# Attention on one Trainium2 core: transposed weights and value products on two shared PSUM buffers, two tiles of queries at a time

## The chip, the cores and the metric

The kernel runs on one core of a Trainium2 chip. The metric is device time in microseconds (us) of that core for one execution of the whole two-layer network; the profile is one further execution, recorded by the hardware profiler. Engines: PE multiplies matrices (PEld is its weight load), DVE is the vector engine, ACT the scalar engine, POOL the general engine, SP issues most DMAs. Each engine runs its instructions in the order of its own queue.

## The reference

Layer 0 is a gated DeltaNet and an S5 scan, layer 1 is attention; a mixture of experts follows each. The change is in the attention of layer 1, which the reference computes so, for three pairs of window and dilation that are merged by their softmax denominators:

```python
scores = einsum('bdnqhe,bdnkhe->bdhnqk', qb, kk) * (e ** -0.5)     # 16 heads of 64, 1024 tokens
scores = where(valid, scores, -1e30)
m = max(scores, -1);  p = exp(scores - m);  ssum = sum(p, -1)
out = einsum('bdhnqk,bdnkhe->bdnqhe', p / ssum, vv);  lse = m + log(ssum)
...
o = einsum('cbsh,cbshe->bshe', softmax(stack(lses)), stack(outs))
y = o @ w_out                                                      # then residual, LayerNorm, experts
```

The kernel merges the three branches into one causal softmax by adding to each score the logarithm of the number of branches that hold the pair (the table `amask`).

## The kernel before

`attention` works on 8 pairs of heads, 8 tiles of 128 queries each, and the two heads of a pair: 128 steps `u`, with a pair's tiles in the order `IORD` = 0, 7, 1, 6, 2, 5, 3, 4. A step with tile `i` has `n = 128 * (i + 1)` keys. The work on PE is written out by hand (`manual_schedule` for PE); the order on the other engines comes from a scheduler that follows a model of the program. Each pass of the loop at L1044 emits:

- `transposed(u)`: the softmax weights `sm` of step `u` (128 queries by `n` keys) are transposed 128 columns at a time (L988) into a PSUM bank `pp`, up to four to a bank. A tile `i > 3` needs two banks full. ACT copies the first to SBUF (`pt`, L992), DVE the second (L994). After each bank come *fillers*: 3 matmuls where `i > 3`, 6 otherwise.
- `out(u - 2)`, at even `u`: the product of values and transposed weights for both heads of a tile (L1007), 2(i + 1) matmuls of 64 columns of weights (the profile has two records for each), into a PSUM bank `po` of its own. ACT copies it to `yt` (L1013); for the last pair ACT and DVE split it into two parts (`olast`, L449 and L450).
- `weights(u + 4)`: scores of step `u + 4` (L965, L967) into a PSUM tile `s`; DVE adds the mask and takes the maximum (L971, L974), ACT exponentiates (L975), DVE divides by the sum (L976, L977).

The fillers are a generator: first the projections of queries and keys of the next pairs (`qk`, L1088, into banks `pj`, with their weight DMAs and copies on ACT, DVE and POOL). They run out in step 108, pair 6. When pair 6 is through (`done`, step 112), the output weights `wo1` are split on ACT and POOL (L1030) with no PE work, and from step 124 on the product with them (L1038) fills again. PSUM has 8 banks, all in use: `s` 2 x 2, `pj` 2, `pp` 1, `po` 1. SBUF tiles `pt` have 3 buffers.

Behind attention, `out_stage` multiplies by `wo1`, normalises and routes; its tables `og`, `ob`, `owr`, `ogb`, `orb` (L191, L233, L236) are loaded by SP. Then 32 experts stream 192 MB of weights (`wraw`, L458), and `combine` ends the program.

Of the kernel before, what the change touches and what calls it, by code (L numbers as in the profile page):

```python
# [10 lines left out]
F32 = mybir.dt.float32  # L11
# [10 lines left out]
NT = 8  # L22
# [29 lines left out]
AH = 4  # L52
# [101 lines left out]
class Trunk:  # L154
# [788 lines left out]
    def attention(self, xTh, xTl, xp, V, ytd, ps, wp):  # L943

        nc = self.nc
        self.banks = {"pj": 2}
        ps.tile([128, D], F32, name="s", tag="s")
        am = wp.tile([128, 1024], F32, name="amask", bufs=1)  # L950
        nc.sync.dma_start(am, self.I["amask"])
        lo_half, hi_half = slice(0, 64), slice(64, 128)
        steps = [(pr, i, a) for pr in range(8) for i in IORD for a in range(2)]
        pairs, P, yts = {}, {}, {}
        with self.pool("at", 2) as ap, self.tc.manual_schedule(engines={mybir.EngineType.PE}):

            def weights(u):
                pr, i, a = steps[u]
                n = 128 * (i + 1)
                QS, KH, KL = pairs[pr]  # L960
                s = ps.tile([128, D], F32, name="s", tag="s")
                w = 256 if n < 256 else 768 if n == 640 else n
                cuts = [0, w] if w <= 512 else [0, 512, w]
                for c0, c1 in zip(cuts[:-1], cuts[1:]):
                    nc.tensor.matmul(s[:, c0:c1], QS[a][:, i * 128:(i + 1) * 128], KH[a][:, c0:c1],  # L965
                                     start=True, stop=False)
                    nc.tensor.matmul(s[:, c0:c1], QS[a][:, i * 128:(i + 1) * 128], KL[a][:, c0:c1],  # L967
                                     start=False, stop=True)
                sm = ap.tile([128, D], F32, name="sm", tag="sm", bufs=AH)
                st = ap.tile([128, 4], F32, name="st", tag="st", bufs=AH + 1)  # L970
                nc.vector.tensor_tensor_reduce(  # L971
                    out=sm[:, :n], in0=s[:, :n], in1=am[:, 1024 - n:1024], scale=1.0, scalar=-3e38,
                    op0=OP.add, op1=OP.max, accum_out=st[:, 0:1])
                nc.vector.tensor_scalar(st[:, 1:2], st[:, 0:1], -1.0, None, op0=OP.mult)  # L974
                nc.scalar.activation(sm[:, :n], sm[:, :n], AF.Exp, bias=st[:, 1:2], accum_out=st[:, 2:3])  # L975
                nc.vector.reciprocal(st[:, 3:4], st[:, 2:3])  # L976
                nc.vector.tensor_scalar(sm[:, :n], sm[:, :n], st[:, 3:4], None, op0=OP.mult)  # L977
                P[u] = sm

            def transposed(u):  # L980
                _, i, a = steps[u]
                sm = P[u]
                pt = ap.tile([128, NT, 128], F32, name="pt", tag="pt", bufs=3)
                for j0 in range(0, i + 1, 4):
                    j1 = min(j0 + 4, i + 1)
                    pp = ps.tile([128, 512], F32, name="pp", tag="pp", bufs=1)
                    for j in range(j0, j1):
                        nc.tensor.transpose(pp[:, (j - j0) * 128:(j - j0 + 1) * 128],  # L988
                                            sm[:, j * 128:(j + 1) * 128], self.ident)
                    v = pp[:, :(j1 - j0) * 128].rearrange("p (j q) -> p j q", q=128)  # L990
                    if j0 == 0:
                        nc.scalar.activation(pt[:, j0:j1], v, AF.Copy)  # L992
                    else:
                        nc.vector.tensor_copy(pt[:, j0:j1], v)  # L994
                    for _ in zip(range(3 if i > 3 else 6), fill):
                        pass
                P[u] = pt

            def out(u):

                pr, i, _ = steps[u]
                if i == IORD[0] and pr < 7:
                    yts[pr] = ap.tile([128, D], F32, name="yt", tag="yt")
                po = ps.tile([128, 512], F32, name="po", tag="o", bufs=1)
                for j in range(i + 1):
                    for a, h in enumerate((lo_half, hi_half)):
                        nc.tensor.matmul(po[h, :128], V[:, j, (2 * pr + a) * 64:(2 * pr + a + 1) * 64],  # L1007
                                         P[u + a][:, j], start=(j == 0), stop=(j == i))
                ts = slice(i * 128, (i + 1) * 128)
                if pr == 7:  # L1010
                    self.split(po[:, :128], O["last"][0][:, ts], O["last"][1][:, ts])
                    return
                nc.scalar.activation(yts[pr][:, ts], po[:, :128], AF.Copy)  # L1013
                if i == IORD[-1]:
                    nc.sync.dma_start(ytd[pr], yts[pr])
                    done.add(pr)

            def fillers():
                yield from self.qk(pairs, xTh, xTl, ap, wp)
                xp.release()  # L1020
                op = O["pool"] = self.tc.alloc_tile_pool(name="ow1", bufs=1, side="right", reuse_waits="tile")
                O["last"] = [op.tile([128, D], F32R, name=f"olast{i}") for i in range(2)]
                while 6 not in done:
                    yield
                raws = [ap.tile([128, D], F32, name="oraw", tag=t) for t in ("QS0", "QS1", "KL1")]
                raw = [raws[k % 3] for k in range(KT)]
                W = O["W"] = []
                for k in range(KT):
                    nc.sync.dma_start(raw[k], self.I["wo1"][k])
                    W.append(self.out_weights(k, raw[k], op, nc.gpsimd))  # L1030
                    yield from [None] * WPACE
                y, yh, yl = (ap.tile([128, KT - 1, 128], F32 if t == "KH0" else F32R, name="y0", tag=t)
                             for t in ("KH0", "KH1", "KL0"))
                nc.sync.dma_start(y, ytd[:, :, 0:128].rearrange("k p t -> p k t"))
                self.split(y, yh, yl)
                O["y"] = [(yh[:, k], yl[:, k]) for k in range(KT - 1)]
                O["po"] = [self.bank("po0", "pj") for _ in range(2)]
                yield from self.out_products(O["po"], O["y"], W, range(KT - 1))  # L1038

            O, done = {}, set()  # L1040
            fill = fillers()
            for _ in zip(range(96), fill):
                pass
            for u in range(-AH, len(steps) + 2):  # L1044
                if 0 <= u < len(steps):
                    transposed(u)
                elif u < 0:
                    for _ in zip(range(6), fill):
                        pass
                if u >= 2 and u % 2 == 0:  # L1050
                    out(u - 2)
                if u + AH < len(steps):
                    weights(u + AH)
            for _ in fill:
                pass
            for _ in self.out_products(O["po"], O["y"] + [[t[:, 0:128] for t in O["last"]]], O["W"], [KT - 1]):
                pass
        return O["W"], O["last"], O["po"], ps, O["pool"]
# [1035 lines left out]
```

## Time and profile before

| | |
|---|---|
| median of 3 runs | 2521.05 us (2517.41 to 2521.86) |
| profiled execution | 2522.76 us, its span 2520.9 us |
| granted TensorE clock, mean | 0.957 of 2.4 GHz |
| PE, DVE, ACT busy over the span | 2276.8, 1466.6, 1146.6 us |
| stretch of the 128 steps | 1364 us to 1781 us |

Times in the rows count from the span's start. A PE row's length holds the pipeline's depth, so that matmuls overlap in the rows: what a matmul costs is the distance from its start to the next one's start.

### The profile page before, as it was taken

How to read it: one execution, taken by the hardware profiler on the slowest of the kernel's cores; microseconds unless marked ns; L12 is line 12 of the kernel's file. 1: busy time of each engine (PE TensorE's matmuls, PEld its weight loads, DVE VectorE, ACT ScalarE, POOL GpSimd, SP SyncE). 2: the span in 40 equal slices, each digit the busy share in tenths (PEclk: the TensorE clock that was granted, in tenths of full speed). 3: DMA queues.
4: the chain of work that ended last, by engine and by line, in shares of the span. 5: the costliest groups of instructions: out<-in, count | busy, mean ns of one | idle time of the engine just before them, and what ended most of it. 6: DMA issues, size and time to landing. Idle time of an engine off the chain costs nothing. (4 is left out here: it accounts for less than half of the span.)

```text
span 2520.9 us, 33905 instructions
## 1 busy us (share of the span) xinstructions
PE 2276.8 (90%) x11950; PEld 1629.8 (65%) x11950; DVE 1466.6 (58%) x2901; ACT 1146.6 (45%) x1871; POOL 485.0 (19%) x566
## 2 busy tenths in 40 slices
PE   7999999899697999998599999997996979999986
PEld 5888888678454555555477777775784545555552
DVE  7655656556853555554554766766468535555545
ACT  5436353442453444443324666666325534444432
POOL 1445433102231111110001111103113311111100
PEclk9999999899798999999799999998997989999997
DMA  4222222272599999999531000102725999999986
GB/s 162 61 64 50 57 79 68 102 272 86 220 365 401 411 404 402 400 399 390 178 124 34 30 31 26 41 24 83 270 74 206 375 398 410 405 405 407 401 334 252
DMA packets 179198, 560.82 MB, mean 222 GB/s; under 512 B 59200, under 2 KB 96448, under 8 KB 129360
## 3 DMA queue, kind: packets, MB, share of 16 engines
q1 hardware_dynamic: 163920, 525.01, 55.1%
q0 software_dynamic: 15104, 33.60, 3.6%
q8 instruction: 96, 1.57, 0.2%
q14 instruction: 78, 0.64, 0.1%
HBM read 518.76 MB, written 55.36 MB: 228 GB/s over the span
## 5 line engine op out<-in xcount | busy, mean ns | idle before, releaser
L489 DVE TENSOR_TENSOR wlo<-wraw,whi 128x1024 fp32r<-128x1024 f32 x380 | 447.8, 1220 | 139.9 <-ACT whi L486 136.9
L486 ACT ACTIVATE whi<-wraw 128x1024 fp32r<-128x1024 f32 x384 | 384.4, 1053 | 76.2 <-PE pu L529 36.2
L583 PE MATMUL pgs<-wraw,xs 128*64 128x512 f32 x1024 | 241.3, 603 | 0.0
L583 PEld LDWEIGHTS pgs<-wraw,xs 128*64 128x64 f32 x1024 | 70.1, 138 | 133.4 <-issue 129.9
L172 PE MATMUL pj<-xTh,phi 128*128 128x512 f32 x320 | 131.9, 417 | 13.6 <-ACT xTh L449 13.6
L1072 POOL TENSOR_TENSOR plo<-praw,phi 128x256 fp32r<-128x256 f32 x64 | 50.2, 786 | 437.6 <-ACT phi L1071 291.4
L172 PE MATMUL pj<-xTh,plo 128*128 128x512 f32 x320 | 132.5, 415 | 0.0
L172 PE MATMUL pj<-xTl,phi 128*128 128x512 f32 x320 | 131.1, 410 | 0.0
L971 DVE CUSTOM_DVE_ANT_0 sm<-s,amask 128x1024 f32<-128x1024 f32 (+7 forms) x128 | 96.6, 756 | 51.5 <-PE s L967 49.6
L528 PE MATMUL pg<-whi,xh 128*128 128x512 f32 x256 | 107.0, 418 | 18.9 <-ACT whi L486 13.8
L599 PE MATMUL pos<-wraw,hs 128*64 128x512 f32 x512 | 118.6, 598 | 5.7 <-ACT xh L449 3.3
L988 PE MATMUL pp<-cf,sm 128*128 128x128 f32 x576 | 100.8, 285 | 22.8 <-ACT pt L992 18.0
L172 PE MATMUL opo<-ohi,oyp 128*128 128x512 f32 x392 | 115.7, 403 | 2.4 <-DVE oyp L450 2.4
L1088 PE MATMUL pj<-xTh,phi 128*128 128x512 f32 x256 | 114.6, 448 | 2.9 <-ACT phi L1071 1.0
L528 PE MATMUL pg<-wlo,xh 128*128 128x512 f32 x256 | 108.2, 423 | 8.1 <-DVE wlo L489 7.8
L551 POOL DMA_INDIRECT yd<-ot,first x32 | 38.0, 1188 | 369.2 <-issue 178.8
L975 ACT ACTIVATE sm<-sm,st 128x1024 f32<-128x1024 f32 (+7 forms) x128 | 99.1, 775 | 18.7 <-DVE st L974 16.4
L988 PEld LDWEIGHTS pp<-cf,sm 128*128 128x128 f32 x576 | 68.4, 143 | 57.8 <-ACT pt L992 50.0
L528 PE MATMUL pg<-whi,xl 128*128 128x512 f32 x256 | 103.4, 404 | 0.0
L529 PE MATMUL pu<-wlo,xh 128*128 128x512 f32 x256 | 102.4, 400 | 0.0
L529 PE MATMUL pu<-whi,xl 128*128 128x512 f32 x256 | 102.3, 400 | 0.0
L529 PE MATMUL pu<-whi,xh 128*128 128x512 f32 x256 | 102.2, 399 | 0.0
(543 smaller groups left out, 5195.7 us busy)
## 6 DMA issues: line engine op xcount, KB each, us to landing
wraw<-in_wm SPq DMA_DIRECT2D x384, 1024.0 KB, 8.3
cy<-yd SPq DMA_DIRECT2D x32, 512.0 KB, 7.3
praw<-in_win SPq DMA_DIRECT2D x40, 256.0 KB, 2.7
oraw<-in_wo SPq DMA_DIRECT2D x16, 512.0 KB, 3.3
hd<-or SPq DMA_DIRECT2D x16, 512.0 KB, 3.2
ca<-hd SPq DMA_DIRECT2D x16, 512.0 KB, 5.9
praw<-in_wqk SPq DMA_DIRECT2D x64, 128.0 KB, 2.3
oy<-ytd SPq DMA_DIRECT2D x14, 448.0 KB, 4.5
```

What stands on the lines that cost most here:

```text
L172: self.last = self.nc.tensor.matmul(*args, **kw).ins
L486: nc.scalar.activation(hi, r[:, h], AF.Copy)
L489: eng.tensor_tensor(lo, r[:, h], hi.bitcast(F32), op=OP.subtract)
L528: nc.tensor.matmul(pg, x[:, k], w[:, 0:512], start=s, stop=z)
L529: nc.tensor.matmul(pu, x[:, k], w[:, 512:1024], start=s, stop=z)
L583: nc.tensor.matmul(pg[r].rearrange("p (g f) -> p g f", g=2), x[:, k], w[:, k % 2, a], start=(k == 0), stop=(k == KT - 1))
L599: nc.tensor.matmul(po[r], hs[:, f % 2, f // 2], W[f // 2][:, o:o + 512], start=(f == 0), stop=(f == 3))
L971: nc.vector.tensor_tensor_reduce(out=sm[:, :n], in0=s[:, :n], in1=am[:, 1024 - n:1024], scale=1.0, scalar=-3e38, op0=OP.add, op1=OP.max, a ...
L975: nc.scalar.activation(sm[:, :n], sm[:, :n], AF.Exp, bias=st[:, 1:2], accum_out=st[:, 2:3])
L988: nc.tensor.transpose(pp[:, (j - j0) * 128:(j - j0 + 1) * 128], sm[:, j * 128:(j + 1) * 128], self.ident)
L1072: nc.gpsimd.tensor_tensor(lo, r, hi.bitcast(F32), op=OP.subtract)
L1088: nc.tensor.matmul(p, w[:, o], x[:, k, cs], start=(k == 0 and i == 0), stop=(k == KT - 1 and i == 2))
```

## The change

`pp` and `po` take two buffers under one name, so that a bank goes to whichever comes next; `pt` gets five buffers; `out` is called for two tiles in a row in every fourth step instead of one in every second.

```diff
@@ transposed(u)
-                pt = ap.tile([128, NT, 128], F32, name="pt", tag="pt", bufs=3)
+                pt = ap.tile([128, NT, 128], F32, name="pt", tag="pt", bufs=5)
...
-                    pp = ps.tile([128, 512], F32, name="pp", tag="pp", bufs=1)
+                    pp = ps.tile([128, 512], F32, name="pp", tag="pp", bufs=2)
@@ out(u)
-                po = ps.tile([128, 512], F32, name="po", tag="o", bufs=1)
+                po = ps.tile([128, 512], F32, name="po", tag="pp", bufs=2)
@@ the loop
-            for u in range(-AH, len(steps) + 2):
+            for u in range(-AH, len(steps) + 1):
...
-                if u >= 2 and u % 2 == 0:
+                if u >= 4 and u % 4 == 0:
+                    out(u - 4)
                     out(u - 2)
```

Lines below the added one move by one (L1088 becomes L1089).

PE, end of pair 0 while there are fillers, before: one product, for tile 5.

```order
L1088 MATMUL pj<-xTl,phi 128x512
L1088 MATMUL pj<-xTh,plo 128x512
L1007 MATMUL po<-pt,V 64x128 x12
L965 MATMUL s<-KH_11959,QS_11957 128x256
L967 MATMUL s<-KL_11961,QS_11957 128x256
L988 MATMUL pp<-cf_58,sm 128x128 [waits Activation_49]
```

The same place after:

```order
L1089 MATMUL pj<-xTl,phi 128x512
L1089 MATMUL pj<-xTh,plo 128x512
L1007 MATMUL po<-pt,V 64x128 [waits DVE_49]
L1007 MATMUL po<-pt,V 64x128 x5
L1007 MATMUL po<-pt,V 64x128 [waits Activation_49]
L1007 MATMUL po<-pt,V 64x128 x11
L965 MATMUL s<-KH_11951,QS_11949 128x256
L967 MATMUL s<-KL_11953,QS_11949 128x256
L988 MATMUL pp<-cf_58,sm 128x128 [waits Activation_49]
```

The product of tile 2 (6 matmuls) has moved here from two steps earlier; each of the two products now waits for a copy out of its bank, the first for DVE's and the second for ACT's.

PE, last pair, between the two kinds of fillers, before: tile 2, and tile 5 follows two steps later.

```order
L988 MATMUL pp<-cf_58,sm 128x128 [waits DVE_49,Activation_49]
L988 MATMUL pp<-cf_58,sm 128x128 x3
L988 MATMUL pp<-cf_58,sm 128x128 [waits Activation_49]
L988 MATMUL pp<-cf_58,sm 128x128
L1007 MATMUL po<-pt,V 64x128 [waits DVE_49]
L1007 MATMUL po<-pt,V 64x128 x5
L965 MATMUL s<-KH_14859,QS_14857 128x512 [waits DVE_49]
```

The same pair after, where both products stand:

```order
L988 MATMUL pp<-cf_58,sm 128x128 [waits DVE_49,PE_49]
L988 MATMUL pp<-cf_58,sm 128x128 x3
L1007 MATMUL po<-pt,V 64x128 [waits Activation_49]
L1007 MATMUL po<-pt,V 64x128 x5
L1007 MATMUL po<-pt,V 64x128 [waits Activation_49]
L1007 MATMUL po<-pt,V 64x128 x11
L988 MATMUL pp<-cf_58,sm 128x128 [waits DVE_49]
```

Here no filler lies between a transpose and the products behind it.

SP, from the last part of attention into `out_stage`, before; the five tables were issued ahead of attention.

```order
L1034 DMA y_15890<-ytd 128x7x128 [waits DMAHW1_49]
L837 DMA ox<-h1d 128x1024 [waits PE_49]
L836 DMA oy<-ytd 128x7x128
L837 DMA ox<-h1d 128x1024
L836 DMA oy<-ytd 128x7x128 [waits DMAHW6_49]
L458 DMA wraw<-in_wm 128x2048 [waits DMAHW7_49,DVE_49]
```

After:

```order
L1034 DMA y_15890<-ytd 128x7x128 [waits DMAHW4_49]
L837 DMA ox<-h1d 128x1024 [waits PE_49]
L836 DMA oy<-ytd 128x7x128
L837 DMA ox<-h1d 128x1024
L836 DMA oy<-ytd 128x7x128 [waits DMAHW1_49]
L191 DMA og<-in_lnmg 128x1024 [waits DMAHW2_49]
L191 DMA ob<-in_lnmb 128x1024 [waits DMAHW3_49]
L233 DMA owr<-in_wr 128x288
L236 DMA ogb<-in_lnm 128x16 [waits DMAHW5_49]
L191 DMA orb<-in_rb 128x36 [waits DMAHW6_49]
```

The two further `pt` buffers take the SBUF in which the tables lay, so their loads now stand behind attention, ahead of the first `wraw`.

## Rows read from the trace of the kernel before

**Rows 1.** Windows by stage: length, busy time of each engine, PEclk, DMA share, GB/s.

```profile
1363.00:1719.00 356.00, 349.36 (x2437) 267.37 (x2436) 247.35 (x681) 228.56 (x515) 42.58 (x53) 1.00 0.09 31
1719.00:1736.00 17.00, 11.63 (x67) 8.55 (x64) 8.68 (x28) 13.22 (x24) 14.53 (x7) 0.70 0.52 194
1736.00:1772.00 36.00, 25.36 (x198) 19.35 (x199) 24.46 (x71) 18.80 (x46) 3.68 (x2) 0.91 0.08 28
1950.00:2400.00 450.00, 414.27 (x1842) 243.35 (x1841) 235.81 (x253) 201.68 (x254) 73.42 (x64) 0.98 1.01 400
```

**Rows 2.** Timeline, one step of tile 4: start, length, engine, instruction, [idle before].

```profile
1516.95 0.60 PE L988 MATMUL pp<-cf,sm 128*128 128x128 f32 x4
1517.31 0.48 PE L1088 MATMUL pj<-xTh,phi 128*128 128x512 f32 x1
1517.62 0.39 PE L1088 MATMUL pj<-xTl,phi 128*128 128x512 f32 x1
1517.65 0.60 ACT L992 ACTIVATE pt<-pp 128x512 f32<-128x512 f32 x1 [1.32 <-PE pp L988]
1517.86 0.40 PE L1088 MATMUL pj<-xTh,plo 128*128 128x512 f32 x1
1518.30 0.14 PEld L988 LDWEIGHTS pp<-cf,sm 128*128 128x128 f32 x1 [0.49 <-ACT pt L992]
1518.30 0.33 PE L988 MATMUL pp<-cf,sm 128*128 128x128 f32 x1
```

**Rows 3.** Waits over 1363 to 1719 us: total, times, longest.

```profile
PEld pp L988 <- ACT pt L992: 30.9, 61, 1.4
PEld po L1007 <- issue: 19.5, 54, 0.4
```

**Rows 4.** Timeline of PE around one product, and two scores without one.

```profile
1678.61 0.40 PE L1088 MATMUL pj<-xTl,phi 128*128 128x512 f32 x1
1678.85 0.39 PE L1088 MATMUL pj<-xTh,plo 128*128 128x512 f32 x1
1679.17 1.31 PE L1007 MATMUL po<-pt,V 128*64 128x128 f32 x20
1680.41 0.39 PE L965 MATMUL s<-KH,QS 128*128 128x256 f32 x1
1680.63 0.28 PE L967 MATMUL s<-KL,QS 128*128 128x256 f32 x1
...
1682.25 0.28 PE L965 MATMUL s<-KH,QS 128*128 128x256 f32 x1
1682.37 0.27 PE L967 MATMUL s<-KL,QS 128*128 128x256 f32 x1
```

**Rows 5.** Timeline of PE: the longest product and the instruction behind it.

```profile
1376.96 1.97 PE L1007 MATMUL po<-pt,V 128*64 128x128 f32 x32
1378.86 0.44 PE L965 MATMUL s<-KH,QS 128*128 128x384 f32 x1
```

**Rows 6.** Groups of instructions, 1719 to 1782 us: busy, mean ns, idle before.

```profile
L988 PE MATMUL pp<-cf,sm 128*128 128x128 f32 x86 | 17.2, 314 | 16.1 <-ACT pt L992 14.8 <-DVE pt L994 1.2
```

**Rows 7.** Timeline of the last pair without fillers, ACT, DVE, POOL and PE.

```profile
1737.65 2.40 POOL L450 TENSOR_TENSOR olo<-oraw,ohi 128x1024 fp32r<-128x1024 f32 x1 [0.36 <-ACT ohi L449]
1738.28 1.91 DVE L977 TENSOR_SCALAR sm<-sm,st 128x256 f32<-128x256 f32 x1
1738.45 0.58 ACT L992 ACTIVATE pt<-pp 128x512 f32<-128x512 f32 x1
1739.08 0.66 PE L988 MATMUL pp<-cf,sm 128*128 128x128 f32 x4 [1.75 <-ACT pt L992]
1740.30 0.35 DVE L977 TENSOR_SCALAR sm<-sm,st 128x256 f32<-128x256 f32 x1
1741.82 0.95 ACT L449 ACTIVATE y<-y 128x896 fp32r<-128x896 f32 x1 [2.79 <-DMA y<-ytd]
```

**Rows 8.** Timeline: the longest wait for a bank, and what ACT did ahead.

```profile
1723.03 1.04 ACT L449 ACTIVATE ohi<-oraw 128x1024 fp32r<-128x1024 f32 x1
1724.09 0.60 ACT L992 ACTIVATE pt<-pp 128x512 f32<-128x512 f32 x1
1724.74 0.47 PE L988 MATMUL pp<-cf,sm 128*128 128x128 f32 x1 [2.43 <-ACT pt L992]
```

**Rows 9.** Timeline, ACT: a product's copy, and a large exponential.

```profile
1503.12 0.28 ACT L1013 ACTIVATE yt<-po 128x128 f32<-128x128 f32 x1 [0.59 <-PE po L1007]
1518.61 1.15 ACT L975 ACTIVATE sm<-sm,st 128x1024 f32<-128x1024 f32 x1 [0.36 <-DVE st L974]
```

**Rows 10.** Timeline from the last product on: SP's first loads, DVE, PE.

```profile
1780.73 0.33 SPq L837 DMA_DIRECT2D ox<-h1d  x1
1782.71 1.56 SPq L458 DMA_DIRECT2D wraw<-in_wm  x2
1787.67 0.45 DVE L241 TENSOR_TENSOR owb<-owr,ogb 128x288 f32<-128x288 f32 x1
1793.47 0.34 PE L244 MATMUL lgW<-osw,cf 128*128 128x72 f32 x2
```

**Rows 11.** Tile `owr`: landing of its two loads.

```profile
DMA to landing us min/median/max: 6.4/6.7/7.0
```

## The prediction

> **What bounds the kernel now.** I read the windows by stage first. While there are fillers (1363 to 1719 us) PE is busy for 349 of 356 us, DVE for 247, ACT for 229: PE sets the pace, and whatever its queue waits for is lost. In the last part (1719 to 1772 us) PE is busy for 37 of 53 us, at a granted clock of 0.70 and 0.91, and the wait that ends last changes between ACT, DVE and a DMA. After that DMA is the bound: its share is 1.01 from 1950 to 2400 us [rows 1]. The first `wraw` is issued at 1782.71, behind the last product [rows 10], so the expert stage cannot have been prefetched earlier; I take it that an end of attention earlier by x brings the end of the kernel forward by x.
>
> The waits and the timeline then say what PE loses. Where a tile fills two banks, its second transposes cannot start until ACT has emptied the only bank. Rows 2 show it: four transposes start at 1516.95, ACT's copy runs from 1517.65 to 1518.25, the next transpose starts at 1518.30. Fillers start 0.23 us apart (1517.62 to 1517.86 is 0.24); from the last filler to the transpose it is 0.44 us, so 0.21 us are lost of the 0.49 us that the weight load waits [rows 2].
>
> **Transposes, one bank more.** In the stretch with fillers the load for a transpose waits 61 times for ACT's copy, 30.9 us in all [rows 3]. Of each wait 0.49 - 0.21 = 0.28 us lie beside a running filler, so 30.9 - 61 x 0.28 = 13.8 us are lost. With two banks the second transposes take the other one, last used a step earlier: 13.8 us go. Late next would be the softmax weights themselves; DVE at 69% and ACT at 64% [rows 1] have room for a stretch that is 6% shorter.
>
> **Products, two in a row.** Matmuls with 64 columns of weights stand between ones with 128. Start to start in rows 4: the last filler to the product is 0.32 us where 0.23 is usual (+0.09). The product has 20 records, and the one of rows 5 has 32: they take 1.24 and 1.90 us up to the scores behind them, so a record costs 0.66 / 12 = 0.055 us and 0.14 us remain that don't depend on the number. The first pair of scores behind it is 0.22 us apart where 0.12 is usual (+0.10) [rows 4, 5]. One visit to the products costs 0.33 us beside the work itself. The stretch has 54 visits [rows 3] and would have 27: 27 x 0.33 = 8.9 us go. The work itself, 36 records for two tiles, stays. The profile gives the wait in front of a product as "issue", that is, it sees no releaser. The Trainium skill (TensorEngine Tiling (Array Packing), Key Properties) says that a change of tiling mode drains TensorE, and that a change of tile inside one mode does not; by that both halves of the price go with the visit and the sum stands, while if the 0.33 us were a hidden wait for `pt`, nothing of them would go and the sum would be 8.9 us higher.
>
> **New waits.** Products and transposes now take turns on two banks. The second product of a group takes the bank of the transposes just ahead of it: between them lie six fillers (1.4 us) and the first product, while copy and landing took 1518.30 - 1516.95 = 1.35 us in rows 2: no wait, unless ACT is in a large exponential, 1.15 us [rows 9]. The transposes behind the group take the bank of the first product. Its copy takes 0.28 us and started 0.59 us after ACT became free for it [rows 9]; the second product alone covers 1.1 to 1.8 us (20 to 32 records at 0.055), scores come on top. Behind these waits PE would hold back the scores of step `u + 4`, for which DVE waits. Bounds: nothing, and 1.15 us in each of the 27 groups, 31 us; nearest are rows 2 and 9, where the cover is longer than the copy, so I take 2 us.
>
> **The last part.** From 1719 us on PE stands idle for 16.1 us in front of transposes, nearly all for copies on ACT [rows 6]. All of these are waits for the bank. But behind them others wait already. one of ACT's copies is late because an output weight is split ahead of it (1.04 us) [rows 8]; ACT stands 2.79 us for a DMA that comes from pair 6's own result, and DVE needs 1.91 us, beside POOL's 2.40 us, for a shape that takes 0.35 us at 1740.30 [rows 7]. None of this goes. And here no filler stands between the transposes and the second product of a group: each of five groups can wait for a copy that starts when ACT is free, about 1.35 us as in rows 2 (7 us in all); in the last pair the product's bank is also held until DVE has read it. So the gain lies between 16.1 us plus five visits (1.7 us), 18 us, and a loss of 7 us; I take the middle of what is left after the new waits, 16.1 + 1.7 - 7 = 11, less 3 us for the stand of rows 7: 8 us.
>
> **Loads behind attention.** The five tables now come after the first two tiles' inputs. `ox` and `oy` twice are 1.9 MB, `og` and `ob` 1 MB, then `owr`; at the 400 GB/s of rows 1 that is 7.4 us from 1780.73, and with a landing of 6.4 to 7.0 us [rows 11] `owr` is there 8 to 10 us after it, at 1789 to 1791 on the old clock. DVE's first use stood at 1787.67, PE's at 1793.47 [rows 10]; the new order has DVE's use behind the row statistics, some 5 us later. Bounds: nothing, and 7 us (a whole landing on PE's queue); nearest are rows 10, so I take nothing. The first `wraw` come 2.9 us later, and these ten loads are far ahead of their use.
>
> **The sum.** -13.8 - 8.9 + 2 - 8 = -28.7 us. The profiled execution took 2522.8 us, 1.7 above the median of the runs; 2522.8 - 28.7 = 2494.1 in the profile, 2492 us against that median.
>
> **Rivals.**
>
> *The last part gives everything back.* All 18 us of it, no new waits, and a clock that stays at 2.4 GHz where it was 1.2 for part of the time because PE then doesn't stand idle: -13.8 - 8.9 - 18 - 3 = -44, 2477 us. For it: every one of the idle rows is a bank. Against it: ACT's and DVE's own delays there [rows 7, 8], and PE there needs only 37 of 53 us.
>
> *The steady gain goes back to ACT's queue.* PE gets ahead, and scores and transposes wait for the softmax or the second product for its bank: only the half of the transposes' term and a little of the last part stay, -12 us, 2509 us. For it: DVE and ACT work in each other's wake, in order. Against it: they have 109 and 127 us of idle time in the stretch [rows 1]. If this took all of it, the time would be 2517 to 2525, no change.
>
> *Slower: the shared banks hold up each group.* A product's copy stands in ACT's queue behind a large exponential (1.15 us) and its own copy (0.28), and the second product behind the transposes' copy: 1.5 us in each of 32 groups is 48 us, against a gain of 22.7 + 8 = 31: 17 us slower, 2538 us. It decides from 31 / 32 = 0.97 us per group on. For it: three users for two banks, and one wait of 2.43 us [rows 8]; against it: in the stretch with fillers the longest wait for a bank is 1.4 us [rows 3], behind a cover of 1.14 us (1516.95 to 1518.09, when the transpose of rows 2 was due), and the new cover is 1.4 us and more. The Trainium skill (Perfetto Trace Analysis, Optimizing Tensor Performance) asks for independent groups on different banks, so that one's copy lies beside the next one's matmuls; the products lose the bank of their own, and by that this rival would be the likelier. Rows 2 against the new order speak the other way.
>
> **How the numbers follow.** Forecast (a gain of 16 to 40 us) 0.68; last part gives everything 0.12; gain goes back, but 6 us or more stay 0.09; no change 0.05; slower 0.06. A change under 0.2%, 5 us, can't be told from none. Faster: 0.68 + 0.12 + 0.09 = 0.89; within 0.2%: 0.05; slower: 0.06. The likeliest case by itself is 2481 to 2505 us; the range for 8 in 10 goes half into its neighbours, 2475 to 2510 us.
>
> **What would show it.** In the profile after: the loads for second transposes start 0.23 us behind the last filler, and the 30.9 us of their wait for ACT are under 5; half as many visits to the products, with 36 records each; the stretch with fillers is some 21 us shorter (335 us); PE's idle time before transposes in the last part about halves, with new waits in front of second products; DMA's full stretch keeps its length and comes earlier by the gain. It would be wrong if a wait of about 1 us appeared in front of each second product or of the transposes behind it, if DVE or ACT stood at 90% there, or if `out_stage` became longer than before.

## The result and the profile after

The changed kernel takes 2486.45 us, the median of four runs (2481.84 to 2489.09); the kernel before took 2519.23 us on the same chip. The ratio is 0.9873, with a 95% interval of 0.9846 to 0.9899: 32.8 us faster. Forecast were 2492 us and a range of 2475 to 2510 us.

The profiled execution after has a span of 2480.0 us, against 2520.9 us before. The difference of 40.9 us is larger than that of the medians: the profiled execution after is the shortest of its four, and the one before (2522.76 us) is longer than its median. The table says where the 40.9 us lie. Three moments split each trace of layer 1: the first transpose of weights, the last filler (projection of the next pair) and the last product. For the two kernels they are the first and last starts in these summaries by line, before:

```profile
L988 PE MATMUL pp<-cf,sm x576: 270/273/475, 1362.5 to 1778.4; 128*128 128x128 f32 x192
L1088 PE MATMUL pj<-xTh,plo x230: 388/397/405, 1349.7 to 1715.6; 128*128 128x512 f32 x115
L1007 PE MATMUL po<-pt,V x1152: 272/273/476, 1370.6 to 1780.4; 128*64 128x128 f32 x192
```

and after:

```profile
L988 PE MATMUL pp<-cf,sm x576: 270/272/331, 1357.9 to 1734.0; 128*128 128x128 f32 x192
L1089 PE MATMUL pj<-xTh,plo x224: 390/395/404, 1350.5 to 1684.9; 128*128 128x512 f32 x112
L1007 PE MATMUL po<-pt,V x1152: 272/273/324, 1370.3 to 1736.8; 128*64 128x128 f32 x192
```

Read in the same way for every kernel that was run (us; the experiments follow below; the kernel before was run again beside each, with medians of 2519.2 to 2521.3 us, so that medians can be set side by side; each ratio is to those runs):

| kernel | up to first transpose | with fillers | last part | behind attention | span | median time |
|---|---|---|---|---|---|---|
| before | 1362.5 | 353.1 | 64.8 | 740.5 | 2520.9 | 2519.2 |
| after | 1357.9 | 327.1 | 51.9 | 743.2 | 2480.0 | 2486.5 |
| e1, banks only | 1363.4 | 333.9 | 53.1 | 743.5 | 2493.9 | 2492.9 |
| e2, grouping only | 1360.1 | 364.5 | 67.1 | 731.3 | 2523.0 | 2528.9 |
| e3, five `pt` only | 1365.3 | 353.5 | 62.7 | 747.3 | 2528.8 | 2524.4 |
| e4, products first | 1359.0 | 327.4 | 52.9 | 725.7 | 2465.0 | 2468.5 |
| e5, e4 with five `pt` | 1360.0 | 327.7 | 53.8 | 740.3 | 2481.8 | 2485.3 |
| e6, after, gather first | 1358.6 | 327.0 | 55.4 | 735.6 | 2476.6 | 2470.8 |
| e7, e4, gather first | 1357.5 | 327.3 | 53.8 | 726.3 | 2465.0 | 2463.2 |
| e8, before, kept busy | 1357.0 | 353.0 | 63.4 | 730.2 | 2503.6 | 2513.9 |
| e9, after, kept busy | 1362.7 | 327.1 | 53.7 | 744.2 | 2487.6 | 2486.8 |

The change takes 26.0 us from the stretch with fillers and 12.9 us from the last part, and gives 2.7 us back behind attention. The 4.6 us ahead of the first transpose are no result: after and e9 are the same program up to there, and their first transposes are 4.8 us apart.

These windows answer to [rows 1] (length, busy time of PE, its weight loads, DVE, ACT and POOL, granted clock, DMA share, GB/s):

```profile
1358.00:1685.00 327.00, 324.63 (x2391) 271.19 (x2390) 246.63 (x676) 221.56 (x508) 44.23 (x52) 1.00 0.09 31
1685.00:1700.00 15.00, 10.81 (x107) 8.35 (x107) 11.43 (x29) 13.14 (x25) 10.96 (x5) 1.00 0.58 207
1700.00:1727.00 27.00, 20.58 (x185) 16.40 (x179) 24.83 (x75) 20.81 (x48) 7.94 (x4) 1.00 0.20 72
1910.00:2360.00 450.00, 414.47 (x1829) 243.05 (x1827) 232.39 (x250) 198.07 (x250) 70.40 (x62) 0.97 1.01 402
```

DVE and ACT do in 327 us nearly what they did in 356, at 75% and 68%. In the last part the granted clock is 1.00 throughout, where it was 0.70 and 0.91. DMA's stretch at a share of 1.01, taken 40 us earlier, has the rate that it had.

A step with two banks, on PE's timeline, as [rows 2] before:

```profile
1643.45 0.60 PE L988 MATMUL pp<-cf,sm 128*128 128x128 f32 x4
1643.81 0.48 PE L1089 MATMUL pj<-xTh,phi 128*128 128x512 f32 x1
1644.13 0.39 PE L1089 MATMUL pj<-xTl,phi 128*128 128x512 f32 x1
1644.36 0.40 PE L1089 MATMUL pj<-xTh,plo 128*128 128x512 f32 x1
1644.60 0.27 PE L988 MATMUL pp<-cf,sm 128*128 128x128 f32 x1
1644.63 0.48 PE L1089 MATMUL pj<-xTh,phi 128*128 128x512 f32 x1
```

The second transpose starts 0.24 us behind the last filler, where it was 0.44. The filler behind it starts 0.03 us later; before, where the transpose had waited, that was 0.09 us (1518.39, the next row of that timeline, less 1518.30). A group of two products, as [rows 4, 5]:

```profile
1650.47 0.40 PE L1089 MATMUL pj<-xTh,plo 128*128 128x512 f32 x1
1650.80 2.19 PE L1007 MATMUL po<-pt,V 128*64 128x128 f32 x36
1652.91 0.38 PE L965 MATMUL s<-KH,QS 128*128 128x256 f32 x1
1653.13 0.28 PE L967 MATMUL s<-KL,QS 128*128 128x256 f32 x1
1653.67 0.33 PE L988 MATMUL pp<-cf,sm 128*128 128x128 f32 x1 [0.25 <-ACT yt L1013]
```

A visit still costs 0.33 us: 0.33 less 0.23 ahead of it, 2.11 less 36 x 0.055 in it, 0.22 less 0.12 behind it. The last row shows the new kind of wait, a transpose that waits for the first product's copy. Over the whole stretch (1358 to 1685 us) it is, for the weight load and for the matmul:

```profile
PEld pp L988 <- ACT yt L1013: 2.7, 6, 0.5
PE pp L988 <- ACT yt L1013: 1.5, 6, 0.3
```

No row of a transpose's load that waits for `pt` is left in that stretch (30.9 us in 61 waits in [rows 3]). In the last part, from 1685 us to the last product, PE's largest waits are now these; before, 14.8 of 16.1 us were for ACT's copy of `pt` [rows 6]:

```profile
PE pp L988 <- DVE pt L994: 3.8, 3, 1.6
PE pp L988 <- ACT yt L1013: 2.8, 2, 1.9
PE po L1007 <- ACT pt L992: 1.0, 2, 0.8
PE pp L988 <- ACT pt L992: 0.8, 1, 0.8
```

### The profile page after: what moved, and what is told of

It reads as the page before. It is cut to its first block, busy times and chain, and to the rows that moved or that the text cites. A ratio compares the mean times of both kernels' runs of the same rounds, so it can differ in the third digit from the quotient of the medians.

```text
span 2480.0 us, 34001 instructions
## 1 busy us (share of the span) xinstructions
PE 2247.2 (91%) x11950; PEld 1629.5 (66%) x11950; DVE 1468.4 (59%) x2901; ACT 1143.1 (46%) x1871; POOL 488.4 (20%) x566
## 5 line engine op out<-in xcount | busy, mean ns | idle before, releaser
L486 ACT ACTIVATE whi<-wraw 128x1024 fp32r<-128x1024 f32 x384 | 384.3, 1054 | 74.6 <-PE pu L529 34.6
L172 PE MATMUL pj<-xTh,plo 128*128 128x512 f32 x320 | 132.2, 414 | 0.0
L528 PE MATMUL pg<-whi,xh 128*128 128x512 f32 x256 | 107.4, 419 | 20.3 <-ACT whi L486 15.2
L1089 PE MATMUL pj<-xTh,phi 128*128 128x512 f32 x256 | 114.8, 448 | 2.2 <-DVE KL L1105 1.0
L528 PE MATMUL pg<-wlo,xh 128*128 128x512 f32 x256 | 108.4, 423 | 8.5 <-DVE wlo L489 8.3
L988 PE MATMUL pp<-cf,sm 128*128 128x128 f32 x576 | 94.0, 274 | 11.7 <-ACT yt L1013 4.3
L528 PE MATMUL pg<-whi,xl 128*128 128x512 f32 x256 | 103.9, 406 | 0.0
L1089 PE MATMUL pj<-xTh,plo 128*128 128x512 f32 x256 | 101.5, 397 | 0.1
```

Of the source, the lines that this page charges most:

```text
L172: self.last = self.nc.tensor.matmul(*args, **kw).ins
L486: nc.scalar.activation(hi, r[:, h], AF.Copy)
L528: nc.tensor.matmul(pg, x[:, k], w[:, 0:512], start=s, stop=z)
L1089: nc.tensor.matmul(p, w[:, o], x[:, k, cs], start=(k == 0 and i == 0), stop=(k == KT - 1 and i == 2))
```

## The experiments

**e1: two shared banks, products as before.** The kernel before with

```diff
-pp = ps.tile([128, 512], F32, name="pp", tag="pp", bufs=1)
+pp = ps.tile([128, 512], F32, name="pp", tag="pp", bufs=2)
-po = ps.tile([128, 512], F32, name="po", tag="o", bufs=1)
+po = ps.tile([128, 512], F32, name="po", tag="pp", bufs=2)
```

> Two shared banks, products still one tile in every second step, pt with three buffers, so the tables stay ahead of attention. Theory (banks and visits are separate prices): the stretch with fillers falls from 353.1 us by 13.8 us of waits for the bank and some 2.7 us of slower starts behind them, to about 337 us; 53 visits to the products stay, each still costing 0.33 us; the last part falls by about 10 of the 12.9 us that the whole change took. In all 25 to 28 us faster than before. Rival (the price of a visit is a hidden wait for a copy): with the second bank it goes as well, and the stretch falls to about 328 us. Rival for the last part (its gain comes from the longer visits, by a clock that does not fall): it falls by 3 us or less.

Measured: 2492.93 us, ratio 0.9885 (0.9865 to 0.9905), 26.7 us faster than before. The stretch with fillers loses 19.2 us, the last part 11.7. So the banks alone give nearly the whole gain of the last part, and grouping adds 6.8 us in the stretch. The 1.2 us that are left in the last part are less than two traces of one order of instructions differ by (see e8 and e9), and the two ratios' intervals overlap.

**e2: grouping alone.** The changed kernel with one bank for `pp` and one for `po` again.

```diff
-pp = ps.tile([128, 512], F32, name="pp", tag="pp", bufs=2)
+pp = ps.tile([128, 512], F32, name="pp", tag="pp", bufs=1)
-po = ps.tile([128, 512], F32, name="po", tag="pp", bufs=2)
+po = ps.tile([128, 512], F32, name="po", tag="o", bufs=1)
```

> Two tiles of products in every fourth step and five pt buffers, but the old banks: one for transposes, one for products. Theory: 27 visits fewer are 9 us less, the waits for the transposes' bank (14 us) stay, and a new wait appears inside each group: the second product waits until ACT has copied the first one's result, about 0.6 us from the first product's end, 27 times, 16 us. The stretch with fillers is 353 - 9 + 16 = 360 us, the last part 3 us longer, the whole 8 to 12 us slower than before. Rival (the price of a visit was a wait for pt that goes on in the group): no 9 us, 369 us in the stretch. Rival (the copy lies beside the second product's weight load): no new wait, 344 us, 9 us faster.

Measured: 2528.87 us, ratio 1.0037 (1.0022 to 1.0051), 9.2 us slower. Its waits from 1360 to 1725 us, of the matmul and of the weight load:

```profile
PE po L1007 <- ACT yt L1013: 19.2, 26, 1.6
PEld pp L988 <- ACT pt L992: 27.0, 54, 1.4
```

The second product of each group waits for the copy of the first out of the only bank, 19.2 us in 26 groups, twice what grouping saves; the transposes' waits are all there. Attention as a whole is 13.7 us slower (11.4 and 2.3 in the table), and the stretch behind attention is 9.2 us shorter; the gather that e4 to e6 are about stands ahead there too. The two spans are only 2.1 us apart (2.4 us lie ahead of the first transpose): e2's profiled execution took 2524.83 us, 4 us less than its median. The number expected came out through deviations that cancelled.

**e3: five `pt` buffers alone.** The kernel before with `bufs=5` on `pt`, which moves the tables' loads behind attention.

```diff
-pt = ap.tile([128, NT, 128], F32, name="pt", tag="pt", bufs=3)
+pt = ap.tile([128, NT, 128], F32, name="pt", tag="pt", bufs=5)
```

> Only the five pt buffers: the tables of the stage behind attention are loaded behind attention. Theory: attention as before (353 us with fillers, 65 us behind), the stage from the last product to the end of the kernel up to 3 us longer, since it was 743.2 us after the change against 740.5 before: 0 to 3 us slower in all. Rival (the longer stage was scatter): nothing. Rival (five buffers by themselves free the transposes): the stretch with fillers is 5 us or more shorter.

Measured: 2524.44 us, ratio 1.0017 (1.0007 to 1.0026), 4.8 us slower. Attention keeps its time (353.5 and 62.7 us). From the last product to the first transpose of the experts it is 138.2 us, as before (138.3), so the late tables hold up nothing. Most of what is added lies at the end, where the last expert's scatter must land before the combination can load its rows (`cy`). SP and GpSimd there:

```profile
2459.38 4.67 SPq L725 DMA_DIRECT2D ca<-hd  x8
2460.30 0.98 POOL L602 DMA_INDIRECT yd<-ots,small  x1 [8.00 <-ACTq L668]
2476.59 12.87 SPq L738 DMA_DIRECT2D cy<-yd  x15
```

The loads of `ca` (eight of 512 KB) begin 0.9 us ahead of the scatter, and `cy` follows it after 16.3 us. Before they begin 8.2 us ahead, and it is 9.0 us. In nine of the eleven kernels it is 8.2 us and 9.0 to 10.1; only e9 is like e3, 0.9 and 16.3. Why `ca` comes late in these two was not found.

**e4: products ahead of the transposes.** The changed kernel with each group of products placed ahead of the transposes of its step, which lets four `pt` do; the tables are then loaded ahead of attention again.

```diff
-pt = ap.tile([128, NT, 128], F32, name="pt", tag="pt", bufs=5)
+pt = ap.tile([128, NT, 128], F32, name="pt", tag="pt", bufs=4)
...
+                if u >= 4 and u % 4 == 0:
+                    out(u - 4)
+                    out(u - 2)
...
-                if u >= 4 and u % 4 == 0:
-                    out(u - 4)
-                    out(u - 2)
```

> The whole change, but a group's two products stand ahead of that step's transposes, which needs four pt buffers and leaves the tables ahead of attention. Theory: fillers of the step before and the scores cover the copies, so the stretch with fillers stays at 327 us (325 to 330); in the last part the second product no longer waits for the copy of the transposes just ahead (2.4 us of such waits were seen), but meets DVE's copy of the step before: 52 us, give or take 3; the stage behind attention is 2 to 3 us shorter. In all 2 to 5 us faster than the change, 35 to 38 us faster than before. Rival (the six fillers between transposes and products were the cover): each of 27 second products waits about 0.5 us, 13 us in all, and the kernel is about 10 us slower than the change.

Measured: 2468.51 us, ratio 0.9792 (0.9772 to 0.9812), 18 us faster than the change. That is more than was foreseen, and none of it is in attention (327.4 and 52.9 us): 17.5 us lie behind it.

PE's waits tell where. GpSimd's queue holds the gathers of the experts' rows (L495) and the sixteen scatters of a table (L428), in the order that the scheduler gave them, and an edit ahead can turn two neighbours round. After the change (start, length, [idle before]):

```profile
1956.49 1.59 POOL L428 DMA_INDIRECT tab<-tokv,place  x1 [0.30 <-issue]
...
1977.72 0.97 POOL L428 DMA_INDIRECT tab<-tokv,place  x1 [0.30 <-issue]
1978.99 1.05 POOL L495 DMA_INDIRECT xg<-hd,small  x1 [0.30 <-issue]
```

In e4:

```profile
1955.40 1.04 POOL L495 DMA_INDIRECT xg<-hd,small  x1 [8.65 <-PE px L503]
1956.86 1.02 POOL L602 DMA_INDIRECT yd<-ots,small  x1 [0.41 <-ACT ots L601]
1958.18 0.98 POOL L428 DMA_INDIRECT tab<-tokv,place  x1 [0.30 <-issue]
```

Counted from the last product, the gather starts at 242.2 us behind the scatters (1978.99 less 1736.8) and at 216.1 us ahead of them (1955.40 less 1739.3). PE waits for it, after the change:

```profile
PE px L503 <- DMA xg<-hd,small: 13.2, 1, 13.2
```

In the kernels so far with the gather behind the scatters (before, after, e1) this wait is 13.2 to 13.4 us; in e2, e3 and e4 the gather stands ahead, and at that place it is 2.1 to 5.0 us. The next two runs ask whether this is the cause.

**e5: e4 with five `pt`.**

```diff
-pt = ap.tile([128, NT, 128], F32, name="pt", tag="pt", bufs=4)
+pt = ap.tile([128, NT, 128], F32, name="pt", tag="pt", bufs=5)
```

> The kernel with the products ahead of the transposes once more, now with the changed kernel's five pt buffers, which puts the loads of the router's tables behind attention again. In the order of GpSimd's queue the sixteen scatters of layer 1's table (L428) now stand ahead of the gather of the seventh expert's rows (L495, small), as they do before the change and after it; in the version with four buffers they stand behind it. Theory 1, the queue: the 13.2 us that TensorE waits for these rows after the change (2.3 us in the version with four buffers) come back, attention stays as it was in that version (327 us with fillers, 53 us in the last part), and the time is that of the changed kernel within 4 us, 2478 to 2486 us. Theory 2, the order of products and transposes, or something it moves in attention, gives the 16 us: 2465 to 2472 us, as with four buffers, though the wait is there.

Measured: 2485.3 us, ratio 0.9868 (0.9852 to 0.9885), 1.2 us from the change. PE's wait is back:

```profile
PE px L503 <- DMA xg<-hd,small: 13.3, 1, 13.3
```

So the order of products and transposes is worth nothing that can be measured, and theory 1 held. The run also brings the tables' loads back behind attention, so by itself it does not part these from the queue; e3 and e6 do. Nor does it part the queue from something else that differs between e4 and e5: the order that the scheduler gave PE, ACT and DVE in the expert stage.

**e6: the change, with the gather ahead of the scatters, in both layers.**

```diff
-        self.nc.gpsimd.indirect_dma_start(
+        self.gath = self.nc.gpsimd.indirect_dma_start(
...
-            if i == 3:
-                with tc.issue_after(st.ins):
+            if i == 5:
+                with tc.issue_after(scat[3].ins), tc.issue_after(self.gath.ins):
                     self.table(l, place)
```

> The changed kernel, with the table's sixteen scatters traced two experts later and queued behind the gather of the seventh expert's rows, in both layers; nothing in attention is touched. Theory 1, the queue: TensorE's two waits for these rows, 14.0 us in layer 0 and 13.2 us in layer 1, go to below 3 us each, and most of it stays to the end: 2454 to 2470 us. Theory 2, the weights' stream takes it back (in the kernel with only five pt buffers a head start of 12 us at the sixth scatter of the experts was 0 us at the last one): the waits go, waits for split or loaded weights take their place, and the time is 2474 to 2484 us.

Measured: 2470.81 us, ratio 0.9799 (0.9776 to 0.9822), 15.6 us faster than the change, with an unusual scatter of 2465.18 to 2478.43. Nothing else was edited, so by the medians this edit is worth most of what e4 had over the change. In layer 1 it also moves PE's, ACT's and DVE's work, but only from 220 to 330 us behind the last product, around the gather. The median falls between the two theories. The profiled execution is the longest of the four (2478.43 us), and its trace shows part of each theory. In layer 0 PE's wait goes from 14.0 us to 3.0 us in two waits, and the sixth expert's scatter from 783.70 to 773.88 us, but the last one stays where it was. After:

```profile
1197.81 0.98 POOL L602 DMA_INDIRECT yd<-ots,small  x1 [7.52 <-ACT ots L601]
```

e6:

```profile
1197.99 0.98 POOL L602 DMA_INDIRECT yd<-ots,small  x1 [7.52 <-ACT ots L601]
```

From 770 to 1200 us PE's waits for split weights (`whi`, L486, in front of L528) rise from 6.8 to 10.1 us: an engine that is ahead meets weights that are not. In layer 1 the last scatter comes 682.2 us behind the last product after the change (2419.01 less 1736.8) and 675.2 us in e6 (2416.23 less 1741.0): half of 14 us is kept. Over all kernels it comes at 678.9 to 682.2 us with the gather behind the scatters (before, after, e1, e5) and at 662.9 to 678.8 us with it ahead (the seven others).

That all of e4's 17.5 us are the queue's is not shown. The 13th expert's scatter, after the change, in e4 and in e6:

```profile
2115.82 1.23 POOL L551 DMA_INDIRECT yd<-ot,first  x1 [4.97 <-ACT whi L486]
2110.12 1.00 POOL L551 DMA_INDIRECT yd<-ot,first  x1 [4.78 <-DVE ot L550]
2111.51 1.23 POOL L551 DMA_INDIRECT yd<-ot,first  x1 [4.98 <-ACT whi L486]
```

Counted from the last product these are 379.0, 370.8 and 370.5 us: up to here e4 and e6 lead the change by the same 8 us. At the last scatter e6 leads by 6.9 us and e4 by 19.3 (2402.16 less 1739.3 is 662.9). The further 11 us of e4 come behind the 13th expert, where PE, ACT and DVE have the same order in e6 as after the change and another one in e4 (of ACT's 392 instructions behind attention 25 stand at another place in e6 and 90 in e4). That this order gives them is a rival that was not tested. Nor does the weights' stream by itself decide it: its last load is issued 650.5 us behind the last product after the change, 647.4 in e4 and 649.7 in e6. What decides how much of the lead stays to the end was not found.

**e7: e4 with the gather ahead in layer 0 too.** The edit of e6 on e4.

> Products ahead of the transposes with four pt buffers, and the table's scatters queued behind the gather in layer 0 too (in layer 1 they are already). Theory 1: layer 0's wait of 14.0 us goes and stays away: 2453 to 2461 us. Theory 2, the weights' stream in layer 0 takes it back: 2465 to 2471 us.

Measured: 2463.24 us, ratio 0.9775 (0.9758 to 0.9791), between the two theories. It is the lowest median, 23 us below the change and 5 us below e4, but the intervals of e4's and e7's ratios overlap. The two spans are the same (2465.0 us), and layer 0 takes its 10 us back as in e6, so the traces show nothing of these 5 us.

**e8 and e9: the clock or the buffers.** PE's clock rose in the last part together with the waits' end, so the last part's 12.9 us could be the clock's. Both kernels got a matmul without a reader at the points where a filler would have stood (102 in all):

```diff
+                def keep():
+                    QS, KH, _ = pairs[7]
+                    nc.tensor.matmul(dm[:, :256], QS[0][:, :128], KH[0][:, :256], start=True, stop=True)
+
                 while 6 not in done:
+                    keep()
                     yield
...
-                    yield from [None] * WPACE
+                    for _ in range(WPACE):
+                        keep()
+                        yield
```

> The kernel before, one bank for transposed weights and one for products, with a matmul of 256 columns added at each of about a hundred points of the last part where a filler would have stood; its result is never read. It is to hold the clock of the last part up (0.80 to 0.85 of 2.4 GHz in the three windows 1715 to 1760 us before, 1.00 after). Theory 1, the buffers: the last part waits for freed banks, which added work neither shortens nor, standing in these waits, lengthens: last part 63 to 70 us (64.8 us before). Theory 2, the clock: most of the 12.9 us that the change takes from the last part are slower matmuls of an engine that waits too much; with the clock up the last part falls to 52 to 58 us. The stretch with fillers stays at 353 us by both. The scatters of the table stand behind the gather here, so the whole time may fall by up to 16 us for that alone; the last part is what is compared.

Measured: 2513.87 us, ratio 0.9971 (0.9959 to 0.9983); the last part is 63.4 us. In its windows the clock (the figure behind POOL's) is 0.97 and 1.00, but for one, and its wait for the bank has halved (14.8 us in [rows 6]):

```profile
1720.00:1735.00 15.00, 12.89 (x93) 10.59 (x93) 9.79 (x23) 11.10 (x22) 14.06 (x6) 0.80 0.49 175
1735.00:1750.00 15.00, 13.48 (x116) 11.40 (x116) 11.36 (x34) 8.66 (x20) 0.00 (x0) 1.00 0.11 32
1750.00:1774.00 24.00, 23.11 (x205) 18.79 (x204) 11.52 (x36) 10.70 (x25) 0.00 (x0) 1.00 0.01 1
```

```profile
PE pp L988 <- ACT pt L992: 7.5, 10, 2.6
```

By the time this is theory 1, yet it does not decide: the added matmuls cost something that a better clock may have paid. The same load on the changed kernel does decide:

> The changed kernel with the same 102 added matmuls of 256 columns in the last part as the kernel before had in the run kept busy, where its last part took 63.4 us at a clock of 0.97, 0.80, 1.00 and 1.00. With both kept busy the clock is no longer what tells them apart. Theory 1, the buffers: most of the 12.9 us between the last parts (64.8 and 51.9 us without the added matmuls) is there still, and the last part takes 51 to 56 us. Theory 2, the clock: the last part takes 60 to 64 us, as the added matmuls cost their own 11 us (102 by 0.107 us between starts at 2.4 GHz), which in the kernel before the better clock paid for.

Measured: 2486.76 us, ratio 0.9865 (0.9825 to 0.9905); the last part is 53.7 us. Two of its windows, at full clock, and its largest waits for a bank from 1690 to 1743 us:

```profile
1685.00:1700.00 15.00, 14.22 (x115) 12.15 (x114) 10.73 (x32) 12.44 (x27) 6.78 (x3) 1.00 0.47 162
1700.00:1715.00 15.00, 12.91 (x117) 11.27 (x117) 13.65 (x35) 12.10 (x24) 12.28 (x6) 1.00 0.52 185
```

```profile
PE pp L988 <- ACT yt L1013: 1.1, 2, 0.9
PE pp L988 <- ACT pt L992: 0.4, 1, 0.4
```

With PE kept busy in both, 63.4 - 53.7 = 9.7 of the 12.9 us are there still. One window of e8 ran at 0.80, so the buffers' share may be somewhat less than 9.7 us, and the clock's somewhat more than 3.2.

Two traces without added work say the same. The last parts of e2 and e6 have the same order of instructions on PE and nearly the same granted clock, but e2 has one bank for each use and e6 two shared ones:

```profile
1724.60:1791.70 67.10, 47.67 (x378) 35.92 (x376) 40.83 (x110) 37.55 (x80) 19.24 (x8) 0.90 0.21 74
1685.60:1741.00 55.40, 44.95 (x378) 36.40 (x376) 41.94 (x110) 37.64 (x80) 19.28 (x8) 0.91 0.26 92
```

Here the banks make 11.7 us. After and e6 have the same banks and the same order on every engine in attention, and clocks of 1.00 and 0.91; they are 3.5 us apart. Single traces scatter, though: before and e3, whose orders in attention are also the same, have 64.8 us at 0.87 and 62.7 us at 0.84. That the buffers are the larger part is shown; the clock's few us are a rough figure.

## Why the prediction was right

- **Bank for the second transposes, -13.8: right.** Summed over the trace, the start of second transposes behind fillers lost 14.2 us before and 0.4 after. The Trainium skill (Perfetto Trace Analysis, Optimization Strategy) says that a gap that repeats on the engine that should be full can mean too few buffers; e1, where one bank more closes these gaps, agrees.
- **Half the visits, -8.9: right.** 53 visits lost 18.6 us over their work, 26 lose 9.1: -9.4. In e1 the 53 visits with two banks lose 19.2 us, so the price belongs to the visit and is no hidden wait for a bank. Nor is it one for `pt`: e3, with five of them, has the row of [rows 3] again, 19.5 us in 54 waits (1366 to 1722 us). By the Trainium skill's rule that a change of tiling mode drains the engine (TensorEngine Tiling (Array Packing), Key Properties) it would be so too; the runs show the price, not the drain.
- **Missed: the slow start behind a wait, -3.** A transpose that waited is followed 0.06 us later than one that did not (0.09 against 0.03 us above); 54 such places are 3.2 us, and e1, without grouping, shows -3.5. The sum counted each wait's length only.
- **New waits, +2 in bounds of 0 to 31: right, a little high.** Six waits, 1.5 us, of which 0.7 us are lost more than before. The cover was argued rightly: six fillers and the first product are longer than a copy. e2 shows what this argument hung on: with one bank for the products each of 26 groups waits, 19.2 us in all. The rival "slower by shared banks" is real, but it belongs to grouping without the second bank. Of the rival in which the gain goes back to ACT's queue these 1.5 us are all there is.
- **Last part, -8 in bounds of -18 to +7: it was -12.9.** This is the term that was mis-sized, as the new waits in it were set at 7 us and the stand on ACT and DVE at 3. In front of products PE waited 1.0 us, not 7; the other 7.4 us of the rows above stand in front of transposes, 2.8 of them for a product's copy and 3.8 for DVE's. With the shorter ones PE's waits fell from 16.0 to 10.7 us, by a third and not by half. These 5.3 us and the five visits' 1.7 leave some 6 us, which must be work that went faster: the clock, which the forecast left out and gave only to a rival, has some 3 us or a little more of them (e8, e9), and the rest was not parted.
- **Tables behind attention, 0 in bounds of 0 to 7: right where it was put.** `out_stage` lasts 139.8 us against 138.3, which the prediction had named as a sign of being wrong; but over all kernels it lasts 137.5 to 139.8 us with the tables ahead of attention and 138.2 to 139.8 with them behind, so the loads are not seen in it. The last expert's scatter comes 3.3 us later from the last product than before, of which 1.5 us are `out_stage` and 1.8 the expert stage; 0.6 us of it are made up behind.
- **"An end of attention earlier by x brings the end forward by x": right here by luck.** Before and after happen to have the same order on GpSimd's queue, and the stretch behind attention differs by 2.7 us only. In seven of the nine experiments that order is the other way, and the stretch behind attention is 5 to 15 us shorter, or 4 to 7 us longer where `ca` comes late as well (e3, e9). Nothing in the prediction foresaw that order.

With what the terms measured, -13.8 - 9.4 - 3.2 + 0.7 - 12.9 + 2.7 = -35.9 us stand against the forecast's -28.7 and the profile's -36.3 (without the stretch ahead of the first transpose); the medians differ by 32.8.

## What to carry to other kernels

Count for each user of a buffer what stands between its release and its next use, on the engine that sets the pace: a second buffer pays where that cover is shorter than the copy, and grouping two uses without it cost more here than it saved. Before a difference in time is put down to an edit, look at every stage: with a scheduler, an edit can turn round two neighbours on a queue far behind it, and turning one such pair in each layer by hand (e6) was worth about half as much as the change. Where a long run of small transfers stands ahead of one that the busiest engine waits for, try that one ahead of them.

## What was not expected of the hardware

- 102 matmuls of 256 columns added to the last part lengthened it by 1.8 us in the changed kernel and by nothing before (-1.4 us), though six of them in a row take 0.89 us from the first to what follows: they stand largely where PE had to wait, and in the kernel before the last part's granted clock rose with them, from 0.87 to 0.95.
- A gather stood 22.5 us behind sixteen scatters of one entry per row (1956.49 to 1978.99), each 1 to 1.6 us on GpSimd with 0.30 us between; 13.2 us of it were PE's wait.
- An advance of 10 us at the sixth of 32 experts in layer 0 was gone at the last one (1197.99 against 1197.81 us), with DMA's share at 1.01 in the stretch between (790 to 1190 us in e6).
